# Half-megabyte weight pieces of two blocks in one staging buffer, and first-norm rows rounded by ScalarE

## The chip, the core and the metric

The kernel runs on one core of a Trainium2 chip. The metric is the device time of one execution in microseconds; three runs of the kernel before gave 1847.68, 1848.91 and 1849.41, median 1848.91. The engines are TensorE (PE, its weight loads PEld), VectorE (DVE), ScalarE (ACT), GpSimd (POOL) and SyncE (SP), which here only issues DMA transfers.

## The reference

One transformer-like block over 256 tokens of width 2048, float32. What matters for this change is its beginning:

```python
mod = (c_act @ ada_w[l] + ada_b[l])[:, None, :]
sh1, sc1, g1, sh2, sc2, g2 = jnp.split(mod, 6, axis=-1)
h = rmsnorm(x, norm1_g[l]) * (1.0 + sc1) + sh1
z = h @ w_in                       # 2048 x 13360: q, the k/v blocks, gates, LRU and merge inputs
q, kc, vc, ks, vs, kw, vw, g_nsa, lx, ly, ga, gb = jnp.split(z, _split_points(), axis=-1)
# sparse attention, a gated recurrence, their merge, a second norm and a conv GLU feed-forward follow
```

`h` needs the scale `1+sc1` and the shift `sh1`, two vectors of 2048, each a product of the 2048-vector `c_act` with a 2048 x 2048 piece of `ada_w`.

## The kernel before

The token axis (256) is the moving side of nearly all matmuls, and width is tiled by 128 rows: 16 K tiles. To keep float32 accuracy, each operand is split into a rounded part `hi` and a rest `lo`, and three products are summed: hi·hi, hi·lo, lo·hi. Weights arrive by DMA in a `raw` buffer of 128 x 2048 floats (1 MB), of which the pool `wpool` has four (L80). `split` (L84) takes 128 x 1024 of it: ScalarE writes `hi` (L88), VectorE writes `lo = raw - hi` (L89). Both have three buffers. A `split` half feeds 24 matmuls of 128 x 256, or 12 of 128 x 512 in the v blocks.

The work around the change is the first part of the input projection: twelve blocks of 512 output columns (four `w_kv`, four `w_q`, two `w_v`, two `w_mq`) over K. The K axis is walked in four spans, `SPANS = ((0,2),(2,6),(6,12),(12,16))` (L26). In each of the first three spans, all twelve blocks multiply the span's K tiles: `q = 0, 1, 2` in the loop at L421. The first two `w_kv` blocks stay in held PSUM banks; the others are added to SBUF after each span (`quad_out`, L355: a ScalarE copy in span 0, a VectorE add later).

Beside this, the rows of `h1` are made for the K tiles to come. `ada1_next` (L259) takes one piece, (m, kt): a 1 MB transfer of `ada_w[m, kt]` into a `raw` buffer, a VectorE multiply with the row of `c` that sums along the row (L272), and a small fix-up (L276 for the scale m = 1, L278 for the shift m = 0). After the shift of tile kt, `norm_mod` makes the rows: VectorE `nt = x * scale * rB` (L251), ScalarE rounds `nt + shift` into the left half of `h1` (L245), VectorE puts the rest into the right half (L246). So each K tile costs two such pieces of `ada_w`, 32 in all. `PACES` (L28) says how many pieces are taken after each weight part: 4 before span 0, 5 in span 0 after its first two tiles, 10 in span 1, 13 in span 2.

In the `w_kv` part of spans 1 and 2, `quad_part` (L345) goes through two K tiles at a time, block by block, so that each load is half a megabyte (two K tiles of one block, 128 x 1024) and takes a `raw` buffer of its own. The same goes for all blocks of span 0, and in span 2 for the last two of the six K tiles of the q, v and mq blocks: 1 MB, then half a megabyte.

Every engine works through its own instructions in order. That order is made when the program is built, by a scheduler that estimates times; `tc.issue_after` and `tc.high_priority` constrain it. SyncE issues the loads in program order: a load whose `raw` buffer is still being read stops all loads behind it.

Of the kernel before, what the change touches and what calls it, by code (L numbers as in the profile page):

```python
# [27 lines left out]
PACES = ('10110101', '1101010110110110', '10110101010111111010')  # L28
# [10 lines left out]
def block_kernel(tc, x_t, cols_d, consts_d, ada_w, w_kv0, w_kv, w_v, w_gate, w_q, cmp_w, cmp_w2,  # L39
# [16 lines left out]
    with ExitStack() as es:  # L56
# [185 lines left out]
        V.tensor_scalar(col("adab", 16, 16), col("adab", 16, 16), 1.0, None, op0=ALU.add)  # L242

# [84 lines left out]
        def quad_banks(q, keep):  # L328
            if keep is None:
                return [bank(), bank()]  # L330
            if q == 0:
                tags = (("s", 2), ("s", 2)) if keep == 0 else (("t", 1), ("o", 1))
                held[keep] = [psx.tile([128, 512], F32, tag=t_, bufs=n_, name="hold") for t_, n_ in tags]
            return held[keep]

        def quad_tiles(ps, hi, lo, c0, kt, first, last):

            for f in range(4):
# [6 lines left out]
        def quad_part(ps, w, k0, k1, first, last):  # L345

            for ka in range(k0, k1, 4):
                kb = min(ka + 4, k1)
                raw = stage(w[:, ka * 512:kb * 512], (kb - ka) * 512)
                for kt in range(ka, kb, 2):  # L350
                    hi, lo = split(raw, (kt - ka) * 512, 1024)
                    for k in range(2):
                        quad_tiles(ps, hi, lo, k * 512, kt + k, first and kt + k == k0, last and kt + k == k1 - 1)

        def quad_out(ps, q, dst, keep):  # L355
            if keep is not None and q < 3:
                return
            for j in range(2):
                v = ps[j].rearrange("p (f t) -> p f t", f=2)
                d = dst[:, 2 * j:2 * j + 2]  # L360
                if q == 0 or keep is not None:
# [4 lines left out]
        def quad(w, q, dst, keep=None):  # L366
            ps = quad_banks(q, keep)
            quad_part(ps, w, *SPANS[q], keep is None or q == 0, keep is None or q == 3)
            quad_out(ps, q, dst, keep)

        def quad_v(b, q):
            ps = [bank(), bank()]
            k0, k1 = SPANS[q]
            for ka in range(k0, k1, 4):
                kb = min(ka + 4, k1)
                raw = stage(w_v[b][:, ka * 512:kb * 512], (kb - ka) * 512)
                for kp in range(ka, kb, 2):
                    hi, lo = split(raw, (kp - ka) * 512, 1024)
                    for j in range(2):
                        for k in range(2):  # L380
                            kt = kp + k
                            xh = h1[:, kt, j * 128:j * 128 + 128]
                            xl = h1[:, kt, 256 + j * 128:256 + j * 128 + 128]
                            wh, wl = hi[:, k * 512:k * 512 + 512], lo[:, k * 512:k * 512 + 512]
                            PE.matmul(ps[j], xh, wh, start=(kt == k0), stop=False, skip_group_check=True)
                            PE.matmul(ps[j], xh, wl, start=False, stop=False, skip_group_check=True)
                            PE.matmul(ps[j], xl, wh, start=False, stop=(kt == k1 - 1), skip_group_check=True)
            for j in range(2):
                if q == 0:
                    A.activation(vN[:, b, j, :], ps[j], AF.Copy)  # L390
                else:
                    V.tensor_tensor(vN[:, b, j, :], ps[j], vN[:, b, j, :], op=ALU.add)
# [8 lines left out]

        def kv_dst(i):
            return kvc[i] if i < 2 else kT[:, i - 2]
# [10 lines left out]
        mq = [big.tile([128, 4, T], F32, tag="M%d" % n, name="mq") for n in range(2)]  # L414
# [5 lines left out]
        keeps = (0, 1, None, None)  # L420
        for q in range(3):  # L421
            if q == 2:
                prepare()
            pss_ = [quad_banks(q, kp) for kp in keeps] 
            if q == 0:

                for kt in range(2):
# [3 lines left out]
                    for half in range(2):  # L431
                        with tc.issue_after(h1_last[1].ins), tc.issue_after(h1_last[half - 1].ins):
                            hi, lo = split(raw, half * 1024, 1024)
                        for i in range(2 * half, 2 * half + 2):
                            quad_tiles(pss_[i], hi, lo, (i % 2) * 512, kt, kt == 0, kt == 1 and i > 1)
# [3 lines left out]
                for i in range(2, 4):  # L439
                    quad_out(pss_[i], 0, kv_dst(i), None)  # L440
            else:
                s0, s1 = SPANS[q]
# [9 lines left out]
            for b in range(2):  # L452
                quad_v(b, q)
                pace(q)
            for i in range(2):
                quad(w_mq[i], q, mq[i])
                pace(q)
# [26 lines left out]
        for i in range(4):  # L484
            quad(w_kv[i], 3, kv_dst(i), keeps[i])
# [5 lines left out]
        for b in range(2):  # L491
            quad_v(b, 3)
# [92 lines left out]
        for i in range(4):  # L585
            quad(w_q[i], 3, qT[i])
# [4 lines left out]
        for i in range(2):  # L591
            quad(w_mq[i], 3, mq[i])
# [270 lines left out]
```

## Time and profile before

| | |
|---|---|
| median of three runs | 1848.91 us |
| the profiled execution | 1850.91 us |
| its span on the core | 1849.1 us |
| PE busy in the span | 1813.8 us (98%) |
| DVE busy | 1400.4 us (76%) |
| ACT busy | 858.2 us (46%) |
| DMA moved | 426.52 MB, mean 231 GB/s |
| DMA busy share, first six fortieths of the span (277 us) | 8 or 7 tenths in most, later 3 to 7 |
| first matmul of span 0, span 1, span 2, span 3 (the scheduler mixes blocks a little) | 20.12, 60.58, 136.07, 250.42 us |

The median is 2.0 us below the profiled execution, and its span is 1.8 us below its own time. A share over the whole span says little about one stage: the first 250 us, with which the change deals, are the ones with the heaviest DMA traffic and nearly all of PE's idle time beyond the start and the end.

### The profile page before, as it was taken

What the parts mean: (1) busy time and instruction counts of PE and PEld (TensorE: products, weight loads), DVE (VectorE), ACT (ScalarE), POOL (GpSimd) and SP (SyncE); (2) the same over time, 40 slices, a digit from 0 to 9 for tenths busy, and PEclk for the clock granted to TensorE, in tenths of its full rate; (3) what the DMA queues carried; (4) which work ended last, traced back from release to release, by engine and by line L of the source; (5) the groups of instructions that cost most, each with busy time, mean ns of one, the idle gap of its engine ahead of it and who ended that gap; (6) DMA issues with size and microseconds to landing.
All of it is one profiled execution on the core that took longest, in us unless ns stands there. A gap on an engine that the chain in (4) does not pass through costs nothing.

```text
span 1849.1 us, 28355 instructions
## 1 busy us (share of the span) xinstructions
PE 1813.8 (98%) x11496; PEld 1616.1 (87%) x11496; DVE 1400.4 (76%) x2074; ACT 858.2 (46%) x1139; POOL 0.2 (0%) x4
## 2 busy tenths in 40 slices
PE   8899999999999999999999999999999999999997
PEld 7798998887899888888888998888888888888887
DVE  7898775888789877877777897888555667676654
ACT  5433343655487544444455544444433444444443
POOL 0000000000000000000000000000000000000000
PEclk9999999999999999999999999999999999999998
DMA  8988873455556777777765566777555555555552
GB/s 327 331 308 327 288 287 137 169 198 204 214 208 231 251 257 276 281 284 284 286 247 205 180 231 230 269 279 277 200 182 185 193 192 183 184 191 194 183 185 89
DMA packets 63060, 426.52 MB, mean 231 GB/s; under 512 B 6993, under 2 KB 7249, under 8 KB 14801
## 3 DMA queue, kind: packets, MB, share of 16 engines
q1 hardware_dynamic: 62928, 424.71, 64.4%
q8 instruction: 90, 1.47, 0.3%
q14 instruction: 42, 0.34, 0.1%
HBM read 422.59 MB, written 2.10 MB: 230 GB/s over the span
## 4 chain that ended last, share of the span: by engine, by line
PE 90%; DMA 4%; DVE 3%; ACT 1%; issue 1%; DVEq 0%; ACTq 0%
PE P L111 40%; PE P L112 21%; DMA raw<-ada_w 3%; PE P L168 3%; PE P L165 3%; PE P L167 3%; PE P L343 2%; PE P L341 2%; PE P L342 2%; PE P L129 1%; PE P L130 1%; PE P L128 1%; DVE lo L89 1%; PE oT L576 1%; PE s L546 1%
## 5 line engine op out<-in xcount | busy, mean ns | idle before, releaser
L88 ACT ACTIVATE hi<-raw 128x1024 fp32r<-128x1024 f32 x593 | 627.6, 1060 | 861.5 <-PE P L111 586.6
L89 DVE TENSOR_TENSOR lo<-raw,hi 128x1024 fp32r<-128x1024 f32 x593 | 723.2, 1222 | 355.6 <-ACT hi L88 354.5
L111 PE MATMUL P<-h,hi 128*128 128x512 f32 x1728 | 600.2, 396 | 0.0
L112 PE MATMUL P<-h,lo 128*128 128x256 f32 x1728 | 468.6, 280 | 0.0
L111 PEld LDWEIGHTS P<-h,hi 128*128 128x128 f32 x1728 | 318.2, 188 | 69.7
L112 PEld LDWEIGHTS P<-h,lo 128*128 128x128 f32 x1728 | 325.9, 189 | 8.4
L111 PE MATMUL P<-ua,hi 128*128 128x512 f32 x480 | 167.0, 394 | 0.0
L341 PE MATMUL P<-h,hi 128*128 128x256 f32 x512 | 146.1, 289 | 6.2 <-ACT hi L88 6.2
L181 DVE SCALAR_TENSOR_TENSOR raw<-raw,crow 128x2048 f32<-128x2048 f32 x64 | 146.3, 2287 | 6.7 <-DMA raw<-ada_w 6.6
L165 PE MATMUL P<-h,hi 128*128 128x256 f32 x512 | 146.8, 287 | 0.7 <-ACT hi L88 0.7
L168 PE MATMUL P<-h,lo 128*128 128x256 f32 x512 | 147.2, 288 | 0.1
L167 PE MATMUL P<-h,hi 128*128 128x256 f32 x512 | 146.8, 287 | 0.0
L342 PE MATMUL P<-h,hi 128*128 128x256 f32 x512 | 144.9, 286 | 0.0
L343 PE MATMUL P<-h,lo 128*128 128x256 f32 x512 | 140.7, 288 | 4.0 <-DVE lo L89 4.0
L112 PE MATMUL P<-ua,lo 128*128 128x256 f32 x512 | 140.2, 280 | 0.0
L341 PEld LDWEIGHTS P<-h,hi 128*128 128x128 f32 x512 | 99.7, 195 | 7.9 <-ACT hi L88 7.6
L111 PEld LDWEIGHTS P<-ua,hi 128*128 128x128 f32 x480 | 88.8, 188 | 19.1
L343 PEld LDWEIGHTS P<-h,lo 128*128 128x128 f32 x512 | 96.3, 194 | 7.3 <-DVE lo L89 5.7
L168 PEld LDWEIGHTS P<-h,lo 128*128 128x128 f32 x512 | 97.9, 191 | 3.3 <-issue 2.5
L165 PEld LDWEIGHTS P<-h,hi 128*128 128x128 f32 x512 | 97.9, 191 | 2.3 <-ACT hi L88 1.3
L342 PEld LDWEIGHTS P<-h,hi 128*128 128x128 f32 x512 | 99.7, 195 | 0.1
L167 PEld LDWEIGHTS P<-h,hi 128*128 128x128 f32 x512 | 97.9, 191 | 1.1 <-issue 1.0
(239 smaller groups left out, 2847.4 us busy)
## 6 DMA issues: line engine op xcount, KB each, us to landing
raw<-ada_w SPq DMA_DIRECT2D x96, 1024.0 KB, 5.0
raw<-w_up SPq DMA_DIRECT2D x96, 1024.0 KB, 4.9
raw<-w_down SPq DMA_DIRECT2D x48, 1024.0 KB, 4.9
raw<-w_lru SPq DMA_DIRECT2D x32, 1024.0 KB, 5.0
raw<-w_proj SPq DMA_DIRECT2D x32, 1024.0 KB, 6.8
raw<-w_gates SPq DMA_DIRECT2D x24, 1024.0 KB, 6.5
raw<-w_out SPq DMA_DIRECT2D x16, 1024.0 KB, 5.0
raw<-w_kv SPq DMA_DIRECT2D x24, 512.0 KB, 6.4
```

Source lines behind the costliest of these rows:

```text
L88: A.activation(hi[:, :n], raw[:, lo_col:lo_col + n], AF.Copy)
L89: V.tensor_tensor(lo[:, :n], raw[:, lo_col:lo_col + n], hi[:, :n].bitcast(F32), op=ALU.subtract)
L111: PE.matmul(ps[f], hi[:, sl], r, start=(kt == 0), stop=False, skip_group_check=True)
L112: PE.matmul(o, lo[:, sl], r[:, 0:256], start=False, stop=(kt == n - 1), skip_group_check=True)
L128: PE.matmul(o, hi[:, sl], r[:, 0], start=(kt == 0), stop=False, skip_group_check=True)
L165: PE.matmul(o, hi[:, sl], r[:, 0:256], start=(kt == 0 and f == 0), stop=False, skip_group_check=True)
L167: PE.matmul(o, hi[:, sl], r[:, 256:512], start=False, stop=False, skip_group_check=True)
L168: PE.matmul(o, lo[:, sl], r[:, 0:256], start=False, stop=(kt == n - 1), skip_group_check=True)
L181: V.scalar_tensor_tensor(raw, raw, 1.0, row, op0=ALU.mult, op1=ALU.mult, accum_out=modc[:, c:c + 1])
L341: PE.matmul(o, hi[:, sl], h1[:, kt, 0:256], start=first and f % 2 == 0, stop=False, skip_group_check=True)
L342: PE.matmul(o, hi[:, sl], h1[:, kt, 256:512], start=False, stop=False, skip_group_check=True)
L343: PE.matmul(o, lo[:, sl], h1[:, kt, 0:256], start=False, stop=last, skip_group_check=True)
```

## The change

- Loads: `part2` stages half a megabyte of each of two neighbouring blocks in one `raw` buffer by two DMAs, then splits and multiplies both halves. It is used for all blocks of span 0, for the `w_kv` blocks of spans 1 and 2, and for the two odd K tiles of span 2 in the q, v and mq blocks (there the pair stands between the two blocks' 1 MB parts; so an odd block multiplies K tiles 10 and 11 first).
- `PACES` is rewritten to the new steps; the totals per span (5, 10, 13) stay. In span 0 it is one piece after each pair (two after the second), in the `w_kv` part of span 1 it is 1, 2, 1, 0 after the four pairs, in that of span 2 it is 1, 2, 1, 1, 1, 0.
- From K tile 2 on, the fix-ups are ScalarE instructions on 128 x 1 (L288, L290 of the new file; `gadd` is made once). `xT` is multiplied by `rB1` in place, for two or four tiles at once (L293). ScalarE makes both the rounded row (L297) and an unrounded copy `nt` (L298); VectorE only subtracts (L299).
- Each piece of `ada_w` and what follows it stands behind the previous K tile's last VectorE instruction (`tc.issue_after(h1_last[1].ins)`).

The numbers of loads, bytes, matmuls and splits are the same. On VectorE 37 instructions fewer are built, on ScalarE 42 more. From span 3 on, all engines' orders are the same as before but for the seam itself, where the small log-sigmoid chain stands (L463 to L482).

```diff
-PACES = ('10110101', '1101010110110110', '10110101010111111010')
+PACES = ('1211', '121011011011', '121110110101010101')
...
+        gadd = const.tile([128, 16], F32, name="gadd")
+        V.tensor_tensor(gadd, col("adab", 16, 16), col("g1", 0, 16), op=ALU.mult)
...
         def ada1_next():
-            if ada1:
+            if not ada1:
+                return
+            with ExitStack() as behind:
+                if h1_last:
+                    behind.enter_context(tc.issue_after(h1_last[1].ins))
                 m, kt = ada1.pop(0)
...
                     V.scalar_tensor_tensor(raw, raw, 1.0, crow, op0=ALU.mult, op1=ALU.mult, accum_out=mc)
                     src = mc
-                with tc.high_priority(200 if kt < 2 else 0):
-                    if m == 1:
-                        V.scalar_tensor_tensor(mc, src, col("adab", 16 + kt), col("g1", kt), op0=ALU.add, op1=ALU.mult)
-                        return
-                    V.tensor_tensor(mc, src, col("adab", kt), op=ALU.add)
-                    h1_last[:] = norm_mod(h1, xT, rB1, 0, 16, kt)
+                if kt < 2:
...
+                elif m == 1:
+                    A.activation(mc, mc, AF.Identity, bias=gadd[:, kt:kt + 1], scale=col("g1", kt))
+                else:
+                    A.activation(mc, mc, AF.Identity, bias=col("adab", kt))
+                    if kt == 2 or kt % 4 == 0:
+                        v = xT[:, kt:kt // 4 * 4 + 4]
+                        V.tensor_tensor(v, v, rB1.unsqueeze(1).to_broadcast([128, v.shape[1], T]), op=ALU.mult)
+                    am = modc[:, 16 + kt:17 + kt]
+                    t = tmp.tile([128, 256], F32, tag="pv1", bufs=2, name="nt")
+                    hi = h1[:, kt, 0:256]
+                    A.activation(hi, xT[:, kt], AF.Identity, bias=mc, scale=am)
+                    ha = A.activation(t, xT[:, kt], AF.Identity, bias=mc, scale=am)
+                    h1_last[:] = ha, V.tensor_tensor(h1[:, kt, 256:512], t, hi.bitcast(F32), op=ALU.subtract)
...
+        def part2(i, pa, pb, q, k0):
+
+            raw = wpool.tile([128, 2048], F32, tag="raw", bufs=4, name="raw")
+            for n in range(2):
+                load(raw[:, n * 1024:n * 1024 + 1024], blocks[i + n][0][:, k0 * 512:k0 * 512 + 1024])
+            for n, ps in ((0, pa), (1, pb)):
+                hi, lo = split(raw, n * 1024, 1024)
+                for k in range(2):
+                    tiles_of(i + n, ps, hi, lo, k * 512, k0 + k, q)
...
-                for k0 in range(s0, s1, 2):
-                    for i in range(4):
-                        quad_part(pss_[i], w_kv[i], k0, k0 + 2, i > 1 and k0 == s0, i > 1 and k0 + 2 == s1)
-                        if k0 + 2 == s1:
-                            quad_out(pss_[i], q, kv_dst(i), keeps[i])
+                for ka in range(k0, k1, 2):
+                    for i in (0, 2):
+                        part2(i, pk[i], pk[i + 1], q, ka)
                         pace(q)
-            for i in range(4):
-                quad(w_q[i], q, qT[i])
+            for i in KV:
+                out_of(i, pk[i], q)
+            for i in range(4, 12, 1 if q == 1 else 2):
+                if q == 1:
+                    whole(i, q)
+                    pace(q)
+                    continue
+                pa = banks_of(i, q)
+                if q == 2:
+                    part(i, pa, q, k0)
+                    pace(q)
+                pb = banks_of(i + 1, q)
+                part2(i, pa, pb, q, k1 - 2)
                 pace(q)
+                out_of(i, pa, q)
+                if q == 2:
+                    part(i + 1, pb, q, k0)
+                    pace(q)
+                out_of(i + 1, pb, q)
```

The loads that SyncE issues for the `w_kv` part of span 1, before: each row without "x2" fills one buffer, each "x2" two buffers.

```order
L53 DMA raw<-w_kv 128x1024
L53 DMA raw<-ada_w 128x2048
L53 DMA raw<-w_kv 128x1024
L53 DMA raw<-ada_w 128x2048
L53 DMA raw<-w_kv 128x1024 x2
L53 DMA raw<-ada_w 128x2048
L53 DMA raw<-w_kv 128x1024 x2
L53 DMA raw<-ada_w 128x2048
L53 DMA raw<-w_kv 128x1024 x2
L53 DMA raw<-ada_w 128x2048
L53 DMA raw<-w_q 128x2048
```

The same place now: each "x2" of `w_kv` fills one buffer together.

```order
L53 DMA raw<-w_kv 128x1024 x2
L53 DMA raw<-ada_w 128x2048
L53 DMA raw<-w_kv 128x1024 x2
L53 DMA raw<-ada_w 128x2048 x2
L53 DMA raw<-w_kv 128x1024 x2
L53 DMA raw<-ada_w 128x2048
L53 DMA raw<-w_kv 128x1024 x2
L53 DMA raw<-w_q 128x2048
```

Thirteen buffers have become eight for the same eight half-megabytes, and one of the five `ada_w` pieces has moved behind the first q block.

ScalarE's order in span 0, where it makes the rows of K tile 2, before. `P` is a PSUM bank that PE fills (of the third and fourth q block here), `nt` what VectorE has made of tile 2.

```order
L362 ACTIVATE qT_162<-P_387 128x512
L245 ACTIVATE h1_131<-nt_425,modc_76 128x256
L362 ACTIVATE qT_162<-P_388 128x512
L88 ACTIVATE hi_471<-raw_469 128x1024
L362 ACTIVATE qT_163<-P_429 128x512
L88 ACTIVATE hi_493<-raw_491 128x1024
```

ScalarE's order there now.

```order
L396 ACTIVATE qT_164<-P_388 128x512
L290 ACTIVATE modc_76<-modc_76,cols_73 128x1
L396 ACTIVATE qT_164<-P_389 128x512
L297 ACTIVATE h1_133<-xbuf_77,modc_76 128x256
L298 ACTIVATE nt_456<-xbuf_77,modc_76 128x256
L88 ACTIVATE hi_475<-raw_472 128x1024
```

One row (L245) has become three (L290, L297, L298), and the first of them stands behind the copy of the third q block's first bank.

VectorE's order at the same place, before: `raw_421` is the shift piece of tile 2, `raw_463` the scale piece of tile 3, `lo_472` the first half of the first v block.

```order
L272 SCALAR_TENSOR_TENSOR raw_421,modc_76<-raw_421,crow_88 128x2048
L89 TENSOR_TENSOR lo_434<-raw_431,hi_433 128x1024
L278 TENSOR_TENSOR modc_76<-modc_76,cols_73 128x1
L272 SCALAR_TENSOR_TENSOR raw_463,modc_76<-raw_463,crow_88 128x2048
L246 SCALAR_TENSOR_TENSOR h1_131<-nt_425,modc_76,h1_131 128x256
L276 SCALAR_TENSOR_TENSOR modc_76<-modc_76,cols_73 128x1
L89 TENSOR_TENSOR lo_472<-raw_469,hi_471 128x1024
```

VectorE's order there now: `raw_451` and `raw_460` are those two pieces, `lo_476` is that half.

```order
L89 TENSOR_TENSOR lo_424<-raw_392,hi_423 128x1024
L278 SCALAR_TENSOR_TENSOR raw_451,modc_76<-raw_451,crow_88 128x2048
L299 TENSOR_TENSOR h1_133<-nt_456,h1_133 128x256
L278 SCALAR_TENSOR_TENSOR raw_460,modc_76<-raw_460,crow_88 128x2048
L89 TENSOR_TENSOR lo_476<-raw_472,hi_475 128x1024
```

The row part of tile 2 (L299) now stands right behind its own shift piece and ahead of the next piece and the next split; it waits for ScalarE's three rows above.

## Rows read from the trace of the kernel before

**Rows 1.** The page's first line.
```profile
span 1849.1 us, 28355 instructions
```

**Rows 2.** Windows by stage: length, then busy time (count) by engine, PE clock, DMA share, GB/s.
```profile
20.00:60.00 40.00, 36.52 (x260) 34.20 (x261) 34.30 (x41) 22.87 (x34) 0.00 (x0) 0.96 0.89 319
60.00:95.00 35.00, 28.97 (x216) 27.28 (x215) 29.46 (x36) 12.07 (x15) 0.00 (x0) 0.95 0.93 344
95.00:138.00 43.00, 43.00 (x318) 41.11 (x318) 41.37 (x53) 17.64 (x18) 0.00 (x0) 1.00 0.82 300
156.00:181.00 25.00, 20.57 (x158) 19.55 (x159) 21.82 (x29) 10.10 (x11) 0.00 (x0) 0.98 0.89 334
181.00:250.00 69.00, 67.59 (x489) 64.38 (x489) 56.58 (x88) 27.09 (x28) 0.00 (x0) 0.98 0.82 297
240.00:260.00 20.00, 20.00 (x169) 20.00 (x168) 15.96 (x38) 8.79 (x10) 0.00 (x0) 1.00 1.01 419
```

**Rows 3.** Waits, 0 to 300 us: who waited for whom, us in total, times, longest.
```profile
DVE raw L272 <- DMA raw<-ada_w: 20.6, 12, 3.7
...
PE P L341 <- ACT hi L88: 6.2, 6, 1.8
...
PE P L343 <- DVE lo L89: 4.0, 8, 0.6
...
PE P L386 <- DVE lo L89: 2.3, 2, 1.4
...
PE hold L341 <- ACT hi L88: 1.3, 1, 1.3
...
PE hold L343 <- DVE lo L89: 0.6, 1, 0.6
```

**Rows 4.** The chain of waits in order of time, 55 to 66 us: start, length, what.
```profile
55.19 7.29 DMA raw<-ada_w
62.50 2.31 DVE raw L272 x2
```

**Rows 5.** PE's timeline where span 0's q blocks begin: start, length, instruction.
```profile
34.41 0.28 PE L341 MATMUL P<-h,hi 128*128 128x256 f32 x1
34.53 0.28 PE L342 MATMUL P<-h,hi 128*128 128x256 f32 x1
```

**Rows 6.** Two short windows, columns as in Rows 2: behind a PE wait, and after it.
```profile
91.50:94.50 3.00, 2.67 (x13) 2.38 (x12) 3.00 (x4) 0.83 (x2) 0.00 (x0) 0.50 1.01 429
95.00:98.00 3.00, 3.00 (x27) 3.00 (x27) 2.82 (x5) 1.98 (x2) 0.00 (x0) 1.00 0.99 382
```

**Rows 7.** VectorE by line, 20 to 138 us: count, busy us, mean ns, idle before.
```profile
L89 DVE TENSOR_TENSOR lo<-raw,hi 128x1024 fp32r<-128x1024 f32 x38 | 45.9, 1221 | 3.1 <-ACT hi L88 2.8
L272 DVE SCALAR_TENSOR_TENSOR raw<-raw,crow 128x2048 f32<-128x2048 f32 x18 | 41.1, 2287 | 7.9 <-DMA raw<-ada_w 7.9
L364 DVE TENSOR_TENSOR qT<-P,qT 128x512 f32<-128x512 f32 x8 | 5.2, 685 | 0.4 <-PE P L343 0.4
L251 DVE SCALAR_TENSOR_TENSOR nt<-xbuf,modc,rB 128x256 f32<-128x256 f32 x9 | 4.3, 481 | 0.1
L246 DVE SCALAR_TENSOR_TENSOR h<-nt,modc,h 128x256 fp32r<-128x256 f32 x9 | 4.3, 480 | 1.2 <-ACT h L245 1.2
L276 DVE SCALAR_TENSOR_TENSOR modc<-modc,cols 128x1 f32<-128x1 f32 x9 | 1.9, 215 | 0.1
L278 DVE TENSOR_TENSOR modc<-modc,cols 128x1 f32<-128x1 f32 x8 | 1.2, 153 | 0.1
```

**Rows 8.** ScalarE by line, whole run.
```profile
L88 ACT ACTIVATE hi<-raw 128x1024 fp32r<-128x1024 f32 x593 | 627.6, 1060 | 861.5 <-PE P L111 586.6 <-PE P L342 66.5 <-PE P L167 41.9
...
L245 ACT ACTIVATE h<-nt,modc 128x256 fp32r<-128x256 f32 x32 | 15.4, 501 | 8.4 <-DVE nt L251 4.6 <-DVE modc L278 3.5
...
L362 ACT ACTIVATE qT<-P 128x512 f32<-128x512 f32 x8 | 4.5, 592 | 0.8 <-PE P L343 0.8
...
L193 ACT ACTIVATE warm<-cols 128x1 f32<-128x1 f32 x1 | 0.2, 203 | 0.0
```

More of the change, by code (lines that the diff above doesn't have):

```diff
@@ L326, in block_kernel, with banks_of, tiles_of @@
         held = {}
-        def quad_banks(q, keep):
-            if keep is None:
+        mq = [big.tile([128, 4, T], F32, tag="M%d" % n, name="mq") for n in range(2)]
+        blocks = [(w_kv[i], kvc[i] if i < 2 else kT[:, i - 2]) for i in range(4)]
+        blocks += [(w_q[i], qT[i]) for i in range(4)]
+        blocks += [(w_v[b], vN[:, b]) for b in range(2)]
+        blocks += [(w_mq[i], mq[i]) for i in range(2)]
+        KV, Q, VB, MQ = range(4), range(4, 8), range(8, 10), range(10, 12)
+        def banks_of(i, q):
+            if i > 1:
                 return [bank(), bank()]
             if q == 0:
[L332 to L336, printed above, removed]
+                tags = (("s", 2), ("s", 2)) if i == 0 else (("t", 1), ("o", 1))
+                held[i] = [psx.tile([128, 512], F32, tag=t_, bufs=n_, name="hold") for t_, n_ in tags]
+            return held[i]
+        def tiles_of(i, ps, hi, lo, c0, kt, q):
+            k0, k1 = SPANS[q] if i > 1 else (0, KT)
+            first, last = kt == k0, kt == k1 - 1
+            if q == 2 and i > 3 and i % 2:
+                first, last = kt == k1 - 2, kt == k1 - 3
+            if i in VB:
+                wh, wl = hi[:, c0:c0 + 512], lo[:, c0:c0 + 512]
+                for j in range(2):
+                    xh = h1[:, kt, j * 128:j * 128 + 128]
+                    xl = h1[:, kt, 256 + j * 128:256 + j * 128 + 128]
+                    PE.matmul(ps[j], xh, wh, start=first, stop=False, skip_group_check=True)
+                    PE.matmul(ps[j], xh, wl, start=False, stop=False, skip_group_check=True)
+                    PE.matmul(ps[j], xl, wh, start=False, stop=last, skip_group_check=True)
+                return
             for f in range(4):
@@ L343, in quad_tiles, with out_of @@
                 PE.matmul(o, lo[:, sl], h1[:, kt, 0:256], start=False, stop=last, skip_group_check=True)
[L345 to L356, printed above, removed]
+        def out_of(i, ps, q):
+            if i < 2 and q < 3:
                 return
             for j in range(2):
-                v = ps[j].rearrange("p (f t) -> p f t", f=2)
-                d = dst[:, 2 * j:2 * j + 2]
-                if q == 0 or keep is not None:
+                dst = blocks[i][1]
+                if i in VB:
+                    v, d = ps[j], dst[:, j]
+                else:
+                    v, d = ps[j].rearrange("p (f t) -> p f t", f=2), dst[:, 2 * j:2 * j + 2]
+                if q == 0 or i < 2:
                     A.activation(d, v, AF.Copy)
@@ L364, in quad_out @@
                     V.tensor_tensor(d, v, d, op=ALU.add)
[L366 to L392, printed above, removed]
@@ new lines, in part @@
+        def part(i, ps, q, k0):
+            raw = stage(blocks[i][0][:, k0 * 512:k0 * 512 + 2048])
+            for kt in range(k0, k0 + 4, 2):
+                hi, lo = split(raw, (kt - k0) * 512, 1024)
+                for k in range(2):
+                    tiles_of(i, ps, hi, lo, k * 512, kt + k, q)
+        def part2(i, pa, pb, q, k0):
[4 more added lines that the diff above has]
+                hi, lo = split(raw, n * 1024, 1024)
+                for k in range(2):
+                    tiles_of(i + n, ps, hi, lo, k * 512, k0 + k, q)
@@ L394, in block_kernel, with whole @@
+        def whole(i, q):
+            ps = banks_of(i, q)
+            part(i, ps, q, SPANS[q][0])
+            out_of(i, ps, q)
         identb = const.tile([128, 128], BF16, name="identb")
@@ L423, in block_kernel @@
                 prepare()
-            pss_ = [quad_banks(q, kp) for kp in keeps]
+            pk = [banks_of(i, q) for i in KV]
+            k0, k1 = SPANS[q]
             if q == 0:
@@ L484, in block_kernel @@
         for i in range(4):
-            quad(w_kv[i], 3, kv_dst(i), keeps[i])
+            whole(i, 3)
             load(xbuf[:, 2048 * i:2048 * i + 2048], cmp_w[i // 2][:, 2048 * (i % 2):2048 * (i % 2) + 2048])
```

28 lines of the change are left out of this document (11 added, 17 removed).

## The prediction, made before the changed kernel was run

> **What bounds the kernel now.** I read the windows by stage first, then the waits, then the chain of waits in order of time, then VectorE by line. The span is 1849.1 us [rows 1], and the change can only move the first 250. In the windows [rows 2] the reader sees PE idle for 40.00 - 36.52 = 3.5 us up to 60, 6.0 us from 60 to 95, nothing from 95 to 138, 4.4 us from 156 to 181 and 1.4 us from 181 to 250, 15.3 together. Nearly all of it has one of two releasers [rows 3]: the next half of weights is not yet rounded (ACT hi: 6.2 + 1.3) or its rest is not yet made (DVE lo: 4.0 + 2.3 + 0.6), 14.4 us in all. The other 0.9 belongs to the first norm, before the change's reach, and stays.
>
> Why are the halves late? The chain [rows 4] shows one turn of a loop: an `ada_w` piece is issued into a `raw` buffer that a split has just freed, lands 7.29 us later, and VectorE reads it for 2.3 us, which frees the buffer again. VectorE waited for such a piece 12 times [rows 3]. The DMA share in those windows is 0.89 to 0.93 at 319 to 344 GB/s, while a stretch with many loads waiting moves 419 [rows 2]. So it is neither bandwidth alone nor VectorE alone (34.3 of 40, 29.5 of 35): the loads start too late because four buffers hold too little.
>
> PE also pays in clock. Behind a wait at 91 us the granted clock is 0.50, the lower level of 1.2 GHz, with 13 matmuls in 3 us; just after, at 1.00, it is 27 [rows 6]. Such a stretch lasts about 3.4 us and costs half of that, 1.7. Over the window from 60 to 95 it shows as 0.95, 5% of 35 us; the two windows on either side of 181 us have 0.98 each, 2% of 25 and of 69 us, which is one more such stretch [rows 2]. Two stretches: 3.4 us. What can be had is 14.4 + 3.4 = 17.8 us, so no less than 1850.9 - 17.8 = 1833.1 on the profiled execution.
>
> **The change part by part: loads.** Count the buffer turns of a `w_kv` part. A turn is landing plus reading, 7.29 + 2.31 = 9.6 us [rows 4], and four run at once. Two matmuls start 0.12 us apart [rows 5], so a half of 24 takes PE 2.88 us. Span 1: before, 8 halves and 5 `ada_w` pieces take 13 turns, 13 / 4 x 9.6 = 31.2 us, against 8 x 2.88 = 23.0 us of PE. Now 4 pairs and 4 pieces: 8 turns, 19.2 us. Span 2: before 12 + 7 = 19 turns, 45.6 us against 34.6; now 6 + 6 = 12 turns, 28.8. Span 0 after its first two tiles: before 8 + 5, 31.2 against 23.0; now 9 turns, 21.6. So before, the turns are over PE in each of the three places, and PE's idle time lies in just these; the excesses (8 + 11 + 8 us) are more than the idle time, since up to three rounded halves in stock, 8.6 us of PE's work, cover a part of each. Now the turns are under PE's time in all three. That is the step on which the forecast rests: the loads cease to be late.
>
> The bandwidth must allow it. Span 1's part moves 8 MB in 23.0 us, 365 GB/s, span 2's 12 MB in 34.6 us, 364; 419 was moved from 240 to 260 us [rows 2]. Span 0 would want 9 MB in 23.0 us, 410 GB/s, so it stays at its limit. A rule speaks against this: the Trainium skill, "DMA: Bandwidth & Descriptors", section "Bandwidth", says that in transfers from HBM the HBM side binds at some 358 GB/s per core. By it, a buffer would take 2.93 us and the parts of spans 0, 1 and 2 26.4, 23.4 and 35.1 us, 4.3 us more than PE's time; with the 2.4 us that I leave in span 0 below counted once, the time would be 1.9 us later than mine, 1840.9, inside the forecast's own range. The 419 of this trace is above that figure, and the trace decides.
>
> **ScalarE and VectorE.** From tile 2 on, VectorE loses per tile 215 + 153 + 481 + 480 = 1329 ns [rows 7]. It gains a subtraction of 128 x 256. That form is not in the trace; it lies between the 153 ns of one column and the 480 ns of the same size with more operands, and from 153 at 1 and 1221 at 1024 columns I take 420. It also gains one two-operand multiply of 128 x 1024 for four tiles, which I put at the 1221 ns of the split (bounds: 685 for half its size from PSUM, 2287 for twice its size): 305 a tile. So VectorE saves 0.60 us a tile, with the bounds 0.9 and 0.3; 4.2 us over the seven tiles made before 138 us, 8.5 us over all fourteen. ScalarE gains two tiny instructions (203 ns each) and one of 501 ns [rows 8] per tile, 0.9 us, 12.7 us in all. It is busy 22.9 of 40, 12.1 of 35, 17.6 of 43 us there [rows 2], so as a sum this is hidden behind its waits.
>
> The order is not free. At tile 2, ScalarE's tiny L290 stands behind a copy that waits for PE's third q half, and VectorE's L299 stands ahead of the next piece and the next split. With the q halves starting at 34.41 [rows 5], the third half's first bank is complete after 2 x 2.88 + 18 x 0.12 = 7.9 us, at 42.3. Then copy 0.59, tiny 0.20, the second bank's copy 0.59 (done 43.7), L297 and L298 0.50 each, L299 0.42: 45.2. Next piece 2.29 to 47.5, split 1.22 to 48.7. PE ends the four q halves at 34.41 + 11.5 = 45.9 and has the rounded part for a few matmuls: it then waits 2.4 us. Before, the waits of this part of span 0 came to about as much (the 3.5 of the first window less 1.1). Span 0 gains nothing, I think.
>
> In span 1, VectorE is the next limit. From the second K pair on, it has 18 splits x 1.22 + 20 adds x 0.685 + 7 pieces x 2.29 + one multiply 1.22 + 3 subtractions x 0.42 = 54.2 us [rows 7], against 20 halves x 2.88 = 57.6 us of PE. That is 94%, and before it was 41.4 of 43 us from 95 to 138 without any PE wait [rows 2]. I leave 1.9 us for the multiply and L299 that now precede span 1's first split (1.22 + 0.42, with handoffs), and 1.5 us for late adds and splits further on. In span 2 the turns have 5.8 us in hand over 34.6, VectorE 2 x 1.22 + 2.29 + 0.42 = 5.15 us a pair against 5.76: I leave 1.3 us at its start, where VectorE comes out of span 1 without any stock.
>
> **The sum.** To be had 17.8; left 2.4 (span 0) + 1.9 + 1.5 (span 1) + 1.3 (span 2) = 7.1, and half of one stretch of low clock, 0.8. Gain 9.9 us: 1841.0 on the profiled execution of 1850.9, which is 2.0 above the median of 1848.9; so 1839.0 for the median. All that follows shifts with it, since the orders behind span 3's seam are the same; there PE was gapless with 419 GB/s from 240 to 260 us, and its loads wait for buffers that PE itself frees, so they come earlier with it.
>
> **Rivals.** *All waits go.* If L299's wait falls together with a DMA wait and VectorE's 94% suffices, only the 0.8 to 2 us of handoffs stay: gain 16 to 17.8, 1831 to 1833. For it: from 95 to 138 us a VectorE at 96% gave no PE wait at all. Against: the walk of span 0.
>
> *VectorE is the bound, and the buffers only move its wait.* Its 12.9 us of idle time from 20 to 138 us (118 less 34.3, 29.5 and 41.4) are only 7.9 of DMA waits [rows 7]; the rest is for ScalarE and PE and would stay or grow. Then the gain is what VectorE no longer does before 138 us, 4.2 us, and nothing in span 2: 1844.7.
>
> *No change.* A pair keeps its buffer until its second half is split, 2.88 us of PE's time after the first, so the turn of a pair is 9.6 + 2.9 = 12.5 us where splits run at PE's pace: spans 1 and 2 then come to 22.1 and 33.1 us, against 23.0 and 34.6, with almost nothing in hand. Every handoff then shows, the buffers give some 2 us in each, and span 0's longer wait on ScalarE takes that back. 1847 to 1850.
>
> *Slower.* One mechanism: ScalarE's rounding now queues behind the fix-ups. Where a piece lands late, VectorE's read, then tiny 0.20, L297 and L298 1.0, only then `hi` 1.06 [rows 8] and `lo` 1.22; before, `hi` ran beside the late piece. This costs 0.20 + 1.0 + 1.06 = up to 2.3 us at each piece that is still late. VectorE waited for 12 of them [rows 3]. If nine stay late, 20.7 us are lost, while a quarter of the 14.4 and VectorE's 4.2 are won: 12.9 us more, 1862. It decides from six late pieces on: 13.8 us against 7.2 + 4.2. Against it: the turns are 6 to 17% under PE's time, so few pieces should be late, and in span 2's `w_kv` part each fix-up stands behind a `hi`.
>
> **How the numbers follow.** Forecast 0.56 (its own range 1834 to 1844), all waits go 0.14, VectorE bound 0.13, no change 0.08, slower 0.09. A measurement can tell 0.2%, 3.7 us, from no change. Faster by more than that means under 1845.2: 0.56 + 0.14 + 0.10 of the VectorE case = 0.80. Within: 0.03 + 0.08 = 0.11. Slower: 0.09. The range starts at the end of the second case, 1831, and takes in the VectorE case with its bounds (savings 0.3 a tile: 2.1 us, 1846.8), so to 1847.5; outside it stay the slower case and part of no change, 0.15.
>
> **What would show it.** The loads are right if ScalarE's waits for `w_kv` and VectorE's for `ada_w` nearly vanish between 60 and 95 and between 156 and 181 us, and PE's idle time there falls from 10.5 to under 5 us. The order is right if VectorE idles 2 to 4 us ahead of L299 near 42 us and PE waits some 2.4 us for the first v half near 46. VectorE's part is right if L299 takes about 0.42 us and L293 about 1.22. Span 3 should begin near 240 us instead of 250.4. I am wrong if it begins after 247, or if PE waits longest for ScalarE's `hi` behind L290 and L298.

## The result and the profile after

| | median (lowest to highest), us | ratio to the runs of before beside it, 95% interval |
|---|---|---|
| before | 1849.16 (1847.68 to 1850.21) | |
| changed | 1831.51 (1831.29 to 1832.09) | 0.9906 [0.9888, 0.9923] |

The changed kernel is 17.7 us faster. The likeliest case of the prediction, 1839.0 (1834 to 1844), was 7.5 us too late; the time is that of the rival "all waits go" (1831 to 1833), which had a chance of 0.14, and lies just inside the whole range. The profiled execution took 1832.09 us. Its span answers to [rows 1]:

```profile
span 1830.3 us, 28370 instructions
```

The stretch that the change can reach ends where PE makes the first gather of span 3 (`cp`). PE's timeline of before has it at

```profile
267.70 0.44 PE L311 MATMUL cp<-gat,xbuf 128*128 128x60 f32 x3
```

and that of the changed kernel at

```profile
249.47 0.44 PE L331 MATMUL cp<-gat,xbuf 128*128 128x60 f32 x3
```

That is 18.2 us earlier; from there to the end of the span it is 1581.4 us before and 1580.8 now. So the whole gain was made ahead of the gather, and what follows only shifts. The windows by stage, to be laid beside [rows 2]:

```profile
20.00:60.00 40.00, 37.68 (x271) 35.63 (x272) 34.46 (x36) 27.09 (x44) 0.00 (x0) 0.96 0.96 362
60.00:95.00 35.00, 33.94 (x279) 33.44 (x279) 32.06 (x34) 17.89 (x25) 0.00 (x0) 1.00 0.96 358
95.00:138.00 43.00, 43.00 (x318) 41.11 (x317) 42.16 (x48) 19.64 (x26) 0.00 (x0) 1.00 0.91 334
138.00:156.00 18.00, 18.00 (x152) 18.00 (x152) 16.83 (x16) 10.62 (x15) 0.00 (x0) 1.00 1.02 397
156.00:181.00 25.00, 25.00 (x210) 25.00 (x210) 22.56 (x25) 11.38 (x15) 0.00 (x0) 1.00 0.93 337
181.00:235.00 54.00, 54.00 (x388) 51.15 (x387) 44.34 (x65) 25.75 (x31) 0.00 (x0) 1.00 0.87 326
```

PE's idle time from 60 to 95 us is 1.06 us instead of 6.0, and from 95 us on there is none, with VectorE busy for 42.16 of 43.00 us. The clock is 1.00 from 60 us on: neither of the two half-clock stretches is left. The DMA engines are fuller where they had holes: 0.96 at 358 to 362 GB/s. The waits, 0 to 300 us (total, times, longest), for [rows 3]:

```profile
ACT hi L88 <- DMA raw<-w_kv: 18.1, 10, 4.7
ACT modc L288 <- DVE raw L278: 6.8, 5, 3.2
DVE h L299 <- ACT nt L298: 4.0, 3, 2.9
DVE raw L278 <- DMA raw<-ada_w: 3.0, 5, 0.9
PE P L375 <- ACT hi L88: 0.7, 1, 0.7
PE hold L382 <- ACT hi L88: 0.5, 1, 0.5
PE hold L384 <- DVE lo L89: 0.5, 1, 0.5
PE P L376 <- DVE lo L89: 0.4, 1, 0.4
```

VectorE's wait for `ada_w` fell from 20.6 to 3.0 us and PE's waits for the weights from 14.4 to some 2.1 (the last four rows). New is the wait of L299 for ScalarE, 2.9 us at the longest. What one PE wait really costs is seen in PE's timeline of the changed kernel around the largest wait of span 1:

```profile
70.64 0.28 PE L383 MATMUL P<-h,hi 128*128 128x256 f32 x1
70.76 0.28 PE L384 MATMUL P<-h,lo 128*128 128x256 f32 x1
71.57 0.39 PE L382 MATMUL hold<-h,hi 128*128 128x256 f32 x1 [0.54 <-ACT hi L88]
71.80 0.28 PE L383 MATMUL hold<-h,hi 128*128 128x256 f32 x1
```

Without it the starts are 0.12 us apart. Here one start is 0.81 us behind the one before it, so 0.69 are lost, and the next stands 0.23 behind that, so 0.11 more: 0.80 us for a wait that the profile books as 0.54, since idle time counts from the modelled end of a matmul (0.28 us after its start).

VectorE by line, 20 to 130 us (count, busy, mean ns, idle before), for [rows 7]; then ScalarE's new rows in the same stretch, for [rows 8]:

```profile
L89 DVE TENSOR_TENSOR lo<-raw,hi 128x1024 fp32r<-128x1024 f32 x38 | 45.5, 1218 | 1.2 <-ACT hi L88 1.2
L278 DVE SCALAR_TENSOR_TENSOR raw<-raw,crow 128x2048 f32<-128x2048 f32 x18 | 41.1, 2285 | 1.8 <-DMA raw<-ada_w 1.8
...
L299 DVE TENSOR_TENSOR h<-nt,h 128x256 fp32r<-128x256 f32 x7 | 2.9, 420 | 4.0 <-ACT nt L298 4.0
...
L293 DVE TENSOR_TENSOR xbuf<-xbuf,rB 128x1024 f32<-128x1024 f32 x2 | 2.4, 1220 | 0.0
```

```profile
L297 ACT ACTIVATE h<-xbuf,modc 128x256 fp32r<-128x256 f32 x7 | 4.2, 599 | 0.2
L298 ACT ACTIVATE nt<-xbuf,modc 128x256 f32<-128x256 f32 x7 | 4.1, 587 | 0.0
L288 ACT ACTIVATE modc<-modc,gadd,cols 128x1 f32<-128x1 f32 x8 | 3.1, 384 | 4.5 <-DVE raw L278 4.5
...
L290 ACT ACTIVATE modc<-modc,cols 128x1 f32<-128x1 f32 x7 | 2.0, 286 | 1.5 <-DVE raw L278 1.5
```

The same 38 splits and 18 pieces now fit into 110 us instead of 118; VectorE waits 1.8 us for pieces in them and not 7.9. Last the buffer turns: SyncE's timeline of before where the `w_kv` part of span 1 begins and where its first q load follows,

```profile
53.82 0.33 SPq L53 DMA_DIRECT2D raw<-w_kv  x1
...
82.26 0.33 SPq L53 DMA_DIRECT2D raw<-w_q  x1
```

and of the changed kernel:

```profile
49.90 0.80 SPq L53 DMA_DIRECT2D raw<-w_kv  x2
...
71.53 0.33 SPq L53 DMA_DIRECT2D raw<-w_q  x1
```

The loads of this part took 28.4 us and take 21.6, with four `ada_w` pieces among them instead of five.

### The profile page after: what moved, and what is told of

Same layout as the page of the kernel before. It is cut to its first block, busy times and chain, and to the rows that moved or that the text cites. A ratio compares the mean times of both kernels' runs of the same rounds, so it can differ in the third digit from the quotient of the medians.

```text
span 1830.3 us, 28370 instructions
## 1 busy us (share of the span) xinstructions
PE 1807.1 (99%) x11496; PEld 1613.3 (88%) x11496; DVE 1394.2 (76%) x2037; ACT 874.4 (48%) x1181; POOL 0.2 (0%) x4
## 4 chain that ended last, share of the span: by engine, by line
PE 95%; DVE 2%; DMA 1%; ACT 1%; issue 1%; SPq 0%; DVEq 0%; ACTq 0%
PE P L111 41%; PE P L112 21%; PE P L165 3%; PE P L168 3%; PE P L382 3%; PE P L384 3%; PE P L167 3%; PE P L383 3%; PE P L129 1%; PE P L130 1%; PE P L128 1%; PE s L577 1%; PE oT L607 1%; PE P L376 1%; PE P L377 1%; PE cp L331 1%
## 5 line engine op out<-in xcount | busy, mean ns | idle before, releaser
L112 PEld LDWEIGHTS P<-h,lo 128*128 128x128 f32 x1728 | 326.4, 189 | 8.3
L168 PEld LDWEIGHTS P<-h,lo 128*128 128x128 f32 x512 | 98.0, 192 | 3.3 <-issue 2.5
L112 PEld LDWEIGHTS P<-ua,lo 128*128 128x128 f32 x512 | 96.6, 189 | 1.8
```

The source lines that it names most:

```text
L112: PE.matmul(o, lo[:, sl], r[:, 0:256], start=False, stop=(kt == n - 1), skip_group_check=True)
L168: PE.matmul(o, lo[:, sl], r[:, 0:256], start=False, stop=(kt == n - 1), skip_group_check=True)
```

## The experiments

The theory: the gain is the buffer turns, of which a shared pair needs one instead of two. Rivals: VectorE's saved time (the modulation), or the new pacing alone. "Gather" is the start of the `cp` matmul above in the profiled execution; from it to the end it is 1580.8 to 1581.4 us in every kernel with four buffers, so it holds all that a change did. But it is one execution, and it varies as the times do: the executions of one kernel lie 0.5 to 7 us apart, and the medians of the kernel before, run beside these, from 1848.8 to 1850.2. So differences of 1 to 2 us between rows are not shown.

| kernel | median, us | ratio, 95% | gather, us |
|---|---|---|---|
| staging and pace, old modulation | 1831.33 | 0.9903 [0.9886, 0.9919] | 247.39 |
| modulation alone | 1852.38 | 1.0011 [1.0001, 1.0021] | 267.95 |
| new kernel, pairs unshared | 1844.13 | 0.9971 [0.9958, 0.9984] | 262.89 |
| pace alone | 1842.55 | 0.9957 [0.9944, 0.9969] | 260.01 |
| staging, old pace | 1832.55 | 0.9909 [0.9894, 0.9923] | 249.95 |
| new kernel, not queued | 1834.37 | 0.9919 [0.9904, 0.9933] | 251.47 |
| new kernel, tiles 2 and 3 as before | 1831.89 | 0.9905 [0.9889, 0.9922] | 249.32 |
| staging, one piece earlier | 1833.06 | 0.9912 [0.9897, 0.9927] | 249.94 |
| staging, two pieces first | 1831.49 | 0.9907 [0.9892, 0.9921] | 248.73 |
| new kernel, three buffers | 1860.95 | 1.0060 [1.0042, 1.0079] | 264.11 |
| before, three buffers | 1892.93 | 1.0242 [1.0227, 1.0257] | 299.76 |
| new kernel, only the multiplies queued | 1831.05 | 0.9898 [0.9882, 0.9915] | 247.86 |

**Which part carries the gain.** Staging alone: the new kernel with the old `ada1_next`.

```diff
...
-                elif m == 1:
-                    A.activation(mc, mc, AF.Identity, bias=gadd[:, kt:kt + 1], scale=col("g1", kt))
...
+                    V.tensor_tensor(mc, src, col("adab", kt), op=ALU.add)
+                    h1_last[:] = norm_mod(h1, xT, rB1, 0, 16, kt)
```

> The changed kernel with the old modulation (VectorE fix-ups, no waiting behind the preceding K tile), the paired buffers and the new pace kept. If the four buffers holding a full megabyte are what made the gain (buffer turns: 19.2 against 23.0 us of PE in span 1's w_kv part, 28.8 against 34.6 in span 2's), nearly all of the 17.7 us stays: 1831 to 1835 us, PE waits after 30 us under 4 us. If VectorE's lighter work (8.5 us over fourteen tiles) is the cause, most of the gain goes: 1839 to 1846 us.

It has the whole gain, so the new modulation adds nothing to it: the medians, 1831.33 without it and 1831.51 with it, cannot be told apart. Behind span 0, one wait of PE longer than 0.2 us is left; its timeline there:

```profile
70.69 0.38 PE L364 MATMUL hold<-h,lo 128*128 128x256 f32 x1 [1.26 <-DVE lo L89]
```

Modulation alone: the kernel before with the new `ada1_next` and `gadd`, old loads and pace.

```diff
...
-                    V.tensor_tensor(mc, src, col("adab", kt), op=ALU.add)
-                    h1_last[:] = norm_mod(h1, xT, rB1, 0, 16, kt)
...
+                    hi = h1[:, kt, 0:256]
+                    A.activation(hi, xT[:, kt], AF.Identity, bias=mc, scale=am)
+                    ha = A.activation(t, xT[:, kt], AF.Identity, bias=mc, scale=am)
...
```

> The kernel before with the new modulation alone, half-megabyte pieces in buffers of their own and the old pace. Buffers as the cause: the loads stay late and VectorE's saving is hidden behind them, 1845 to 1850 us. VectorE as the cause: 1836 to 1842 us. If ScalarE's longer queue is the price that the pairs hide, it is slower than before: 1851 us or more.

No gain, rather 0.1% the other way. Its windows show where VectorE's saved time went: VectorE is less busy (32.58 and 28.83, against 34.30 and 29.46 in [rows 2]) and PE as idle as before.

```profile
20.00:60.00 40.00, 36.22 (x253) 33.72 (x254) 32.58 (x34) 24.83 (x40) 0.00 (x0) 0.95 0.87 314
60.00:95.00 35.00, 29.04 (x225) 27.20 (x224) 28.83 (x30) 15.35 (x24) 0.00 (x0) 1.00 0.95 348
```

Pairs unshared: the new kernel, each half-megabyte in a buffer of its own.

```diff
-            raw = wpool.tile([128, 2048], F32, tag="raw", bufs=4, name="raw")
-            for n in range(2):
-                load(raw[:, n * 1024:n * 1024 + 1024], blocks[i + n][0][:, k0 * 512:k0 * 512 + 1024])
+            raws = [stage(blocks[i + n][0][:, k0 * 512:k0 * 512 + 1024], 1024) for n in range(2)]
```

> The changed kernel with each half of a pair in a raw buffer of its own: order of loads, pace and modulation as changed, only the sharing undone. Buffers as the cause: 12 turns in span 1's w_kv part, 12 / 4 x 9.6 = 28.8 us against 23.0 of PE, and 18 in span 2's, 43.2 against 34.6; the time goes back to 1843 to 1849 us. If the order or the modulation is the cause, it stays within 3 us of the changed kernel: 1831 to 1835 us.

Order, pace and modulation are the new ones, and yet the gather comes 13.4 us later than in the changed kernel, and the median is 12.6 us higher. The shared buffer alone is worth that. By the spacing of matmul starts, some 4.5 us of it are stretches at half the clock, which come back here.

Pace alone: the kernel before, with one piece of span 1 and one of span 2 dealt out later.

```diff
-PACES = ('10110101', '1101010110110110', '10110101010111111010')
+PACES = ('10110101', '1101010011110110', '10110101010011111110')
```

> The kernel before with one piece of ada_w moved out of the w_kv part of span 1 and one out of that of span 2 (behind the first q block and the first v block), all else as before. By buffer turns each part loses one of its turns, 9.6 / 4 = 2.4 us: 1843 to 1847 us. If the loads are not what bounds these parts, 1848 to 1850 us.

The gather is 7.7 us earlier, more than one turn fewer in each part gives (2 x 2.4 us). But the two half-clock stretches of the kernel before are gone as well, and they cost 2.7 us by the spacing of matmul starts; the other 5.0 are about what the turns give. Its windows:

```profile
60.00:95.00 35.00, 31.45 (x251) 30.22 (x250) 29.93 (x37) 14.13 (x17) 0.00 (x0) 1.00 0.96 349
156.00:181.00 25.00, 24.23 (x198) 23.62 (x197) 19.91 (x23) 9.84 (x11) 0.00 (x0) 1.00 0.93 322
```

Is that worth additive? The staging alone with the pieces as early as before:

```diff
-PACES = ('1211', '121011011011', '121110110101010101')
+PACES = ('1211', '121110110110', '121111110100010101')
```

> The new kernel with the modulation as before (like the run of the staging alone, 1831.3) and with the ada_w pieces dealt out as early as in the kernel before: 5 pieces in the w_kv part of span 1 and 7 in that of span 2, where the new kernel has 4 and 6. Theory (buffer turns): 9 and 13 turns of 9.6 us over four buffers are 21.6 and 31.2 us, still under the 23.0 and 34.6 us that PE needs, so little comes back: 1831 to 1835, and no stretch at half the clock in the middle. Rival (the pace has a worth of its own, as its 6.6 us in the kernel before suggest): most of the 6.6 us come back, 1836 to 1839.

The turn theory holds: against the staging alone, the old pace costs 2.6 us of the gather and 1.2 of the median here, not 7.7. Pace and sharing relieve the same shortage, so their worths (7.7 for the pace alone, 17.8 for the staging with the old pace) do not add up.

**Does the count of turns hold in size?** Both kernels with one buffer fewer, at each place where one is taken; the first of them:

```diff
-            raw = wpool.tile([128, 2048], F32, tag="raw", bufs=4, name="raw")
+            raw = wpool.tile([128, 2048], F32, tag="raw", bufs=3, name="raw")
```

> The new kernel with three raw buffers instead of four, in the whole kernel; it is read by the first gather of span 3 (249.5 us in the new kernel, 267.7 in the kernel before), since all before it is the stretch of the change. Theory (a turn is 9.6 us whatever the number of buffers): 9, 8 and 12 turns over three buffers are 28.8, 25.6 and 38.4 us against PE's 23.0, 23.0 and 34.6, 12.2 us too much; by the same count the kernel before had 27.3 us too much and lost 22.4, so 10 us are lost here: the gather starts near 259, and half-clock stretches come back. Rival (landing time is queueing, and with a quarter fewer bytes under way a load lands in about 5.5 us instead of 7.3, so a turn is 7.8): 23.4, 20.8 and 31.2 us, hardly over PE: 250 to 253. From span 3 on I expect 0 to 10 us more in either case.

> The kernel before with three raw buffers instead of four, read by the same gather (267.7 us with four). Theory (turn 9.6 us): 13, 13 and 19 turns over three buffers are 41.6, 41.6 and 60.8 us, 63 us more than PE needs; at the share of before (22.4 of 27.3) some 52 us are lost instead of 22: near 297. Rival (landing falls with the bytes under way, to a turn of 7.8): 33.8, 33.8 and 49.4 us, 36.4 too much, 30 us lost: near 275.

The kernel before came near the theory (299.8, expected 297), in part by luck: its turns were shorter than 9.6 us (below), and its clock was lower, 0.90 from 60 to 95 and 0.86 from 156 to 181 us (0.95 and 0.98 with four buffers). The new one lost 14.6 us instead of 10, and the half-clock stretches that I had expected did not come: its clock is 1.00 from 60 us on. Both also need some 14 us more behind the gather, which I had put at 0 to 10 for the new one. SyncE's timeline gives the turns; the new kernel with three buffers,

```profile
53.84 0.80 SPq L53 DMA_DIRECT2D raw<-w_kv  x2
...
80.65 0.33 SPq L53 DMA_DIRECT2D raw<-w_q  x1
```

and the kernel before with three:

```profile
61.73 0.33 SPq L53 DMA_DIRECT2D raw<-w_kv  x1
...
97.79 0.33 SPq L53 DMA_DIRECT2D raw<-w_q  x1
```

26.8 us for 8 turns over three buffers is 10.1 us a turn; 36.1 us for 13 is 8.3. With four buffers the same count gives 10.8 (21.6 us for 8) and 8.8 (28.4 us for 13), though in the changed kernel PE hardly waits, so there its pace may set the turn. The median landing of all loads from 45 to 180 us bears on the rival: the changed kernel with four buffers, then with three,

```profile
DMA to landing us min/median/max: 3.9/7.2/9.0
```

```profile
DMA to landing us min/median/max: 3.6/6.2/7.8
```

Landing does fall with fewer buffers, by 1.0 us of the 1.8 that the rival supposed, and in the kernel before by 1.4 (6.8 to 5.4). So neither side is right: a turn is not the same whatever the number of buffers, and it did not fall to 7.8 either. Followed one by one in the new kernel with three buffers, from a pair's issue to that of the next load into the same buffer, the four pairs of this part turn in 9.8, 11.0, 8.3 and 8.8 us. Each buffer came free when the second half was split, 2.5 to 3.4 us after that half had landed; the 9.6 had counted 2.3 for this.

**The wait that is left in span 0.** The order put L299 behind ScalarE's copy of PE's third q half. ScalarE's timeline of the changed kernel, then VectorE's:

```profile
42.64 0.60 ACT L396 ACTIVATE qT<-P 128x512 f32<-128x512 f32 x1 [1.56 <-PE P L384]
43.13 0.28 ACT L290 ACTIVATE modc<-modc,cols 128x1 f32<-128x1 f32 x1
43.36 0.60 ACT L396 ACTIVATE qT<-P 128x512 f32<-128x512 f32 x1
43.85 0.59 ACT L297 ACTIVATE h<-xbuf,modc 128x256 fp32r<-128x256 f32 x1
44.34 0.59 ACT L298 ACTIVATE nt<-xbuf,modc 128x256 f32<-128x256 f32 x1
```

```profile
44.97 0.42 DVE L299 TENSOR_TENSOR h<-nt,h 128x256 fp32r<-128x256 f32 x1 [2.91 <-ACT nt L298]
45.31 2.29 DVE L278 SCALAR_TENSOR_TENSOR raw<-raw,crow 128x2048 f32<-128x2048 f32 x1
```

Behind it PE loses about 2.0 us at 47 to 49 us, by the spacing of starts around these two waits:

```profile
47.36 0.98 PE L375 MATMUL P<-hi,h 128*128 128x512 f32 x2 [0.69 <-ACT hi L88]
48.79 0.50 PE L376 MATMUL P<-lo,h 128*128 128x512 f32 x1 [0.45 <-DVE lo L89]
```

Three runs took this wait apart. First without the queueing of the pieces:

```diff
-                if h1_last:
-                    behind.enter_context(tc.issue_after(h1_last[1].ins))
```

> The new kernel without the queueing of each ada_w piece behind the previous K tile's last VectorE instruction; all else as in the new kernel. VectorE's order then has all four in-place multiplies of xT by rB1 (0.68 + 3 x 1.22 = 4.3 us) ahead of the rows of K tile 0. Theory (the queueing only keeps the order of VectorE): PE's first matmul of span 0 comes some 4 us later, and as the spans behind run without waits the whole does too: 1835 to 1836. Rival (VectorE waits for its first pieces there, so the multiplies are hidden): 1831 to 1832.

The multiplies moved to the start as expected, and PE's first matmul of span 0 came 5.2 us later (25.38; 20.21 in the changed kernel). PE's waits there:

```profile
PE hold L380 <- ACT h L247: 8.4, 1, 8.4
```

But the gather came only 2.0 us later: from there on PE has no wait at all. That the late start left time to fill the buffers is the likely reason, which no run shows. Both theories missed this; the time, 1834.37, lies between them. PE's first matmul of the q blocks, here and then in the changed kernel, gives a measure for later: to the gather it is 211.27 us here and 214.95 there (233.29 in the kernel before, whose q blocks begin at 34.41 [rows 5]).

```profile
40.20 0.28 PE L380 MATMUL P<-h,hi 128*128 128x256 f32 x1
```

```profile
34.52 0.28 PE L382 MATMUL P<-h,hi 128*128 128x256 f32 x1
```

Second, K tiles 2 and 3 as before:

```diff
-                if kt < 2:
-                    with tc.high_priority(200):
+                if kt < 4:
+                    with tc.high_priority(200 if kt < 2 else 0):
...
-                    if kt == 2 or kt % 4 == 0:
+                    if kt % 4 == 0:
```

> The new kernel with the rows of K tiles 2 and 3 made on VectorE as before; from tile 4 on as in the new kernel. Theory (PE's loss of some 2.0 us at 47 to 49 us comes from VectorE's wait of 2.9 us for ScalarE's copies ahead of L299): that loss goes, 1829.4 to 1830.3, and the only large wait left is near 71 to 73 us. Rival (VectorE is as loaded there, and its 2 x 0.9 us of more work and its own wait for ScalarE's rounded row put the loss back): 1831 to 1833.

The rival held in the time: the loss at 47 us fell to about 1.0, but 0.6 came up at 60 us. So who computes the row is at most a part of the cause. VectorE stood idle there too, 1.35 us, with the piece behind it still queued.

Third, only the in-place multiplies queued:

```diff
-                if h1_last:
+                if h1_last and ada1[0][1] < 3:
...
+                        with tc.issue_after(h1_last[1].ins):
+                            V.tensor_tensor(v, v, rB1.unsqueeze(1).to_broadcast([128, v.shape[1], T]), op=ALU.mult)
```

> The new kernel with only the in-place multiplies of xT queued behind the previous K tile's last VectorE instruction; the ada_w pieces from K tile 3 on are not. VectorE's order at tile 2 then has the next piece (2.3 us) ahead of the subtraction that waits for ScalarE's copies, as the run of the staging alone has it, while the multiplies do not move to the start. Theory (the 2.0 us that PE loses at 47 to 49 us in the new kernel come from VectorE standing idle 2.9 us in that wait, which the queueing of the next piece causes): VectorE waits under 1 us there, PE's loss at 47 to 49 goes or falls under 0.7, the first gather of span 3 comes at 247.4 to 248.3 instead of 249.5, and the time is 1829.4 to 1830.5. Rival (the next piece has not landed by then, or the loss only moves to 71 to 73 us): gather at 249 to 250, 1831 to 1832.

VectorE's timeline there, with the next piece in the place of the wait:

```profile
41.12 2.29 DVE L278 SCALAR_TENSOR_TENSOR raw<-raw,crow 128x2048 f32<-128x2048 f32 x1
...
44.10 0.42 DVE L300 TENSOR_TENSOR h<-nt,h 128x256 fp32r<-128x256 f32 x1 [0.69 <-ACT nt L299]
```

The wait is 0.69 us, and the gather at 247.86 is 1.6 us earlier; but 0.9 of that lie ahead of the first q block (33.66 us here), before the wait. PE's loss near 47 us fell to 0.8, not under 0.7; the loss near 71 us, 1.6 in the changed kernel, stayed at 1.5. The place is as the theory has it, the time is not: the median, 1831.05 (1830.45 to 1831.82), overlaps with the runs of the changed kernel. It beats the kernel before, and is not shown to beat the changed one.

**The last wait of span 1** (1.4 us at 70.7 in the staging alone). One piece moved into span 0, then two pieces put first:

```diff
-PACES = ('1211', '121011011011', '121110110101010101')
+PACES = ('1212', '111011011011', '121110110101010101')
```

> The staging alone (1831.3) with one ada_w piece taken from behind the second w_kv pair of span 1 and put at the end of span 0, so that the third pair's load stands behind one piece and not two. Theory (the one wait left there, 1.4 us at 70.7 us, is that pair landing late): it goes, 1829.7 to 1830.2. Rival (span 0 then has 10 turns, 24.0 us against PE's 23.0, and the wait only moves to the end of span 0): 1831 to 1833.

```diff
-PACES = ('1211', '121011011011', '121110110101010101')
+PACES = ('1211', '211011011011', '121110110101010101')
```

> The staging alone (1831.3) with the ada_w pieces of span 1's w_kv part as 2, 1, 1, 0 instead of 1, 2, 1, 0 behind the four pairs: the third pair's load stands behind one piece, the second's behind two. Theory (the wait of 1.4 us at 70.7 us is the third pair behind two pieces in SyncE's order): it goes or halves, 1829.7 to 1830.8, unless the second pair is then late. Rival (two pieces cost the same wherever they stand, and the wait moves one pair ahead, near 62 us): 1831 to 1832.

In both the rival held: the wait moved to 58.8 and 60.4 us (2.8 us together) and to 64 to 66 us (2.1 us). In the first a half-clock stretch came with it, as the window's clock shows:

```profile
60.00:95.00 35.00, 34.64 (x276) 34.64 (x277) 30.91 (x38) 14.27 (x15) 0.00 (x0) 0.95 0.90 339
```

## Why the prediction was right in kind and too small in size

- *The loads cease to be late*: right, and the whole of the gain. Sharing alone (13.4 us against the unshared pairs) and the staging without the modulation (all of it) show it. In the two windows that the prediction named (60 to 95 and 156 to 181 us), ScalarE's waits for `w_kv` fell from 21.8 to 2.1 us and VectorE's for `ada_w` from 9.6 to 0.9. The turn of 9.6 us was a fair mean: where turns bind, 8.3 to 10.1 us were measured.
- *What can be had, 17.8 us*: too small, and the first mis-sized term. From the first q block to the gather PE took 233.29 us before, and 211.27 in the run that was not queued, where it never waited there: 22.0 us could be had, 4.2 more. By the spacing of matmul starts the two half-clock stretches are 2.7 of them, where I put 3.4; the other 19.3 are the 18 waits with the matmul behind each, where I put their booked idle time, 14.4.
- *What stays, 7.1 + 0.8 us*: the other one; by the same measure 3.7 us stayed (214.95 - 211.27). Span 0's walk was right: L299 was to end at 45.2 and ended at 45.39, VectorE idled 2.9 us (2 to 4), PE lost 2.0 (2.4). The 1.9 for span 1's start were near in size by luck: the multiply and L299 ahead of the first split made PE wait for nothing there (0.2 us near 60 us). What PE lost is 1.6 us, 12 us later, at the third pair, which landed late (ScalarE's line below); I had no term for that. The 1.5 for later adds and splits, the 1.3 at span 2's start and the 0.8 of clock were all zero. I charged an engine at 94% for handoffs; at 98%, from 95 to 138 us, it made PE wait for nothing. 22.0 - 3.7 = 18.3, against the 18.2 of the gather; 4.2 more to be had and 4.2 less left explain the 8.4 between this and my 9.9. ScalarE ahead of the third pair's first half:

```profile
70.46 1.06 ACT L88 ACTIVATE hi<-raw 128x1024 fp32r<-128x1024 f32 x1 [1.70 <-DMA raw<-w_kv]
```

- *VectorE saves 0.60 us a tile*: the durations were right (L299 420 ns, L293 1220), the worth is nil, as the modulation alone and the staging alone show. *ScalarE gains 0.9 us a tile*: 1.36 by the rows (384 + 286 + 599 + 587, less the 501 of L245); hidden all the same. The Trainium skill, "ScalarE: Activation LUTs", section "What ACT_TABLE_LOAD costs", adds some 93 ns for each operand that is a pointer to a column; the 599 and 587 ns against 501 agree, and I had overlooked that scale and bias are now both columns.
- *The rule that speaks against the change* (the Trainium skill, "DMA: Bandwidth & Descriptors", section "Bandwidth": the HBM side binds at some 358 GB/s per core): not borne out here. From 138 to 156 us the core moved 397 GB/s and PE had no wait.
- *The rivals*: "no change" and "slower" fell. The first had a pair's turn at 12.5 us, and in the changed kernel the four pairs of span 1's `w_kv` part do turn in 11.4 to 11.7 us; but PE hardly waits there, and with three buffers, where loads were late, they turned in 8.3 to 11.0. So a long turn alone does not tell that buffers bind. The mechanism of "slower" was there (ScalarE's L288 waited for VectorE, 6.8 us in five times), but VectorE waited only 3.0 us for pieces, and no `hi` cost PE a booked wait of more than 0.7 us. The time is that of "all waits go", but by luck: 3.7 us stayed, not its 0.8 to 2, and 22.0 could be had, not 17.8.

Left open: why waits of much the same length lose the clock in one kernel and not in another (2.2 us of idle time at 152 us with three buffers did not, 1.6 and 0.8 at 59 and 60 us in the run with one piece earlier did). A fifth buffer was not tried.

## What to carry to other kernels

When loads are late with the DMA engines below their best rate, count the turns of the staging buffers (landing plus the time until they are read) against the compute time of the stage; a half-filled buffer costs a whole turn. Price a wait of PE by the spacing of matmul starts, not by its booked idle time, and do not charge leftovers for an engine that is only nearly full while there is rounded stock ahead of it. An instruction queued behind another that waits makes the wait idle time: leave the next independent piece free to fill it (here this took PE's loss behind the wait from 2.0 to 0.8 us, and the time no further than its spread).

## What the runs showed of the hardware

- A short PE wait cost some 0.27 us more than the profile books: 0.16 between the spacing of starts (0.12) and a matmul's modelled length (0.28), 0.11 in the matmul behind it (0.80 for a booked 0.54 at 71.57 us).
- Loads landed sooner with fewer buffers under way: a median of 7.2 us with four buffers of 1 MB and 6.2 with three; in the kernel before, 6.8 and 5.4.
- Small ScalarE instructions on 128 x 1 are far from free: 286 ns with one column operand (L290), 384 with two (L288).
